# A two-layer hybrid backbone in one kernel: the MLPs' way down moved between the pairs of the way up, its gated adds moved to accumulating DMAs, and a padded layout for the convolution

## The chip, the core and the metric

One core of a Trainium2 chip runs the whole kernel. The metric is the device time of one execution in microseconds (us). Before the change it is 2623.2 us, the median of 3 runs (2618.38 to 2624.76).

Engines are named as the profile names them: PE (TensorE, matmul), PEld (its weight load), DVE (VectorE), ACT (ScalarE), POOL (GpSimd) and SP (SyncE, which issues most DMAs).

## The reference, cut to what matters

640 tokens (128 of a prompt, 512 of a latent grid) of width 1024 pass two layers. Each layer is a block of three mixers, which the change leaves alone, and a gated MLP of inner width 2816:

```python
xn2 = rmsnorm(x, norm2) * (1 + scale2) + shift2
u = dwconv3(xn2 @ w_up, ffn_conv_w)           # width 3 over positions, prompt and grid apart
a, bval = u[..., :D_FF], u[..., D_FF:]
x = x + gate2 * ((jax.nn.silu(a) * bval) @ w_down)
```

After the second layer a last rmsnorm gives the output.

## The kernel before, in words

**Layout.** Channels lie on the 128 partitions, the 640 tokens (T) along the free axis, in two halves of 320 (HALF), since one matmul fills 320 columns of a PSUM bank. Every f32 operand is split in two parts, `hi` and `lo` (ACT casts `hi`, L116; DVE subtracts for `lo`, L117), and a product takes three matmuls for each block of 128 x 128 weights: hi·hi, hi·lo, lo·hi (L149 to L151, L473 to L475). A weight tile `wraw` or `T` (128 x 512: four blocks) is loaded on SP's queue and split into `whi` and `wlo`, of which 6 are kept (`WB`).

**The way up** makes 22 pairs of a gate and a value column block (`NFF`). A pair would take 8 products of half the depth (4 blocks) by half the tokens, 96 matmuls; `pair_steps` (L477) does it in 7, 84 matmuls, by a scheme of sums of weights (L497) and sums of activations (`T3`, `t2`, `T4`, `t1`, made once for each MLP by `Forms.second`, L442). `B11`, `B21` are the first token half of the normalised input (made by `Forms.first` while the layer's output projection still runs), `B12`, `B22` the second. The pieces are collected from PSUM banks `Y`, `X`, `Z` into `o` and `z` (ACT copies L504, L523, L529, L534, L543; DVE adds L513, L531, L535). Then `ffn_conv` (L966) makes the convolution (one ACT product L968, then on DVE two taps for each of two segments, L970 and L972), and `ffn_act` (L976) silu, product and split into `fh`, `fl`.

**The way down** runs in 4 parts (`FFPARTS`: pairs 0 to 4, 5 to 10, 11 to 16, 17 to 21). When a part's pairs, and the first pair of the next part, are done, all 8 output blocks m of that part follow in one piece: `product` into a bank from `ps.any()`, then `add_gated` (L560 to L563) adds gate times product to `x[m]` on DVE, in 3 instructions for each m. The last part is done by token halves, with the squares for the next norm and the next norm's steps (`first`) between. The first 3 pairs (`LEAD`) do their `B11` and `B21` products ahead, since those need the first token half only.

**In layer 0** `ada_rows` (L308) also runs in the MLP: 12 loads of rows of `w_ada`, each with two long DVE products (L320).

**Order.** A scheduler orders each engine's instructions by when they can run in its own model and by the order in the code, and gives out the buffers. Each engine then runs its list strictly in order. The scheme's first waits are therefore set by where a `wlo` split stands in DVE's list.

Of the kernel before, what the change touches and what calls it, by code (L numbers as in the profile page):

```python
# [16 lines left out]
P = 128  # L17
# [28 lines left out]
DMA_ADDS = False  # L46
LEAD = 3
# [3 lines left out]
FFPARTS = ((0, 5), (5, 11), (11, 17), (17, 22))  # L51
# [6 lines left out]
def hybrid_flow_kernel(ctx: ExitStack, tc: tile.TileContext, a: dict):  # L58
# [109 lines left out]
    class ps:  # L168
# [4 lines left out]
        BUFS = {"mla": {"sc": 2, "pt": 2}, "hgrn": {"sc": 2, "m": 1, "ad": 1}, "ffn": {"Y": 2, "Z": 2, "X": 2}}  # L173
# [37 lines left out]
        @staticmethod  # L211
        def any():

            ps.turn += 1
            tag = ("lin", "X", "Z", "Y")[ps.turn % 4]
            return (ps.bank() if tag == "lin" else ps.one(tag))[:, 0:HALF]
# [192 lines left out]
    class Forms:  # L409


        def __init__(self, l, which, sq, xf):
            self.l, self.which, self.sq, self.xf = l, which, sq, xf
            self.f = {n: [None, None] for n in ("B11", "B21", "B22", "t1", "t2", "T3", "T4")}
            self.raw = {}

        def put(self, name, q, f):
            if name in ("t2", "T3", "T4"):
# [23 lines left out]
        def second(self, pool):  # L442
            bc = self.sq.rstd(1)
            raw = self.raw
            for q in range(2):
                for n, name in enumerate(("B12", "B22")):
                    f = raw[name, q] = form_tile(pool, F32, "fh", "xn", 7)
                    for e in range(2):
                        norm_raw(self.l, self.which, self.sq, 1, f, e, KH * n + 2 * q + e, bc)
                f = raw["T3", q] = form_tile(pool, F32, "fl", "xs", 7)  # L450
                V.tensor_tensor(f, raw["B22", q], raw["B12", q], ALU.subtract)
                self.put("T3", q, f)
            for q in range(2):
                f = raw["t2", q] = form_tile(pool, F32, "fl", "xs", 7)
# [10 lines left out]
            for q in range(2):  # L465
                self.put("B22", q, raw["B22", q])
# [10 lines left out]
    def pair_steps(l, g, F, pool, lead, banks, evict):  # L477
# [3 lines left out]
        def load(src, own=False):  # L481
            t = (pool.tile([P, 512], F32, tag="T", name="T", bufs=LEAD) if own else
# [10 lines left out]
        def add(t, src, tile=None):  # L493
            if DMA_ADDS:
                G.dma_start(t, src, accum_op=ALU.add)
            else:
                V.tensor_tensor(t, t, tile, ALU.add)  # L497

        h0, h1 = half(0), half(1)
        o0 = pool.tile([P, T], F32, tag="o", name="o", bufs=4)  # L500
        t = load(wa, True)
        Y = banks[0]()
        part_product(Y, form(t), F.operand("B11"), True, False)
        S.copy(o0[:, h0], Y)  # L504

        rb = None

        def second():
            nonlocal rb
            rb = load(wb)  # L510
            X = banks[1]()
            part_product(X, form(rb), F.operand("B21"), True, True)
            V.tensor_tensor(o0[:, h0], X, o0[:, h0], ALU.add)  # L513
        if lead:
            second()
        yield
        o1 = pool.tile([P, T], F32, tag="o", name="o", bufs=4)
        rc = load(wc)
        add(t, wc, rc)
        Z = banks[2]()  # L520
        part_product(Z, form(t), F.operand("T3"), True, False)
        z = pool.tile([P, HALF], F32, tag="z", name="z", bufs=2)
        S.copy(z, Z)  # L523
        if not lead:
            second()
        rd = load(wd)
        add(t, wd, rd)
# [4 lines left out]
        add(rc, wd, rd)  # L532
# [433 lines left out]
    def ffn_conv(g, o, fp, fconv):  # L966
        u = fp.tile([P, T], F32, tag="u", name="u", bufs=3)
        S.mul(u, o, fconv[:, 1, g:g + 1])  # L968
        for s0, s1, s in ALLSEGS:
            V.scalar_tensor_tensor(u[:, s0 + 1:s1], o[:, s0:s1 - 1], fconv[:, 0, g:g + 1], u[:, s0 + 1:s1],  # L970
                                   ALU.mult, ALU.add)
            V.scalar_tensor_tensor(u[:, s0:s1 - 1], o[:, s0 + 1:s1], fconv[:, 2, g:g + 1], u[:, s0:s1 - 1],  # L972
                                   ALU.mult, ALU.add)
        return u

    def ffn_act(ua, ub, fp):  # L976
        S.activation(ua, ua, AF.Silu)
# [84 lines left out]
    for l in range(DEPTH):  # L1062
# [126 lines left out]
        with pool_of("fp") as fp:  # L1189
# [12 lines left out]
            def up_pair(j):
                us = {}

                def evict(s, o):
                    us[s] = ffn_conv(s * NFF + j, o, fp, fconv)
                    if s == 0:
                        Ys.append(ffn_act(us[0], us[1], fp))
# [171 lines left out]
```

## Time and profile before

| | |
|---|---|
| median of 3 runs | 2623.2 us (2618.38 to 2624.76) |
| the profiled execution: its own time, its span | 2630.3 us, 2628.5 us |
| PE busy, share of the span | 2505.1 us, 95% |
| DVE busy | 1948.2 us, 74% |
| ACT busy | 1239.4 us, 47% |
| POOL busy | 117.7 us, 4% |
| granted clock of PE, mean | 0.981 |

A window's row says: its stretch in us from the span's start, its length, then busy us (and instructions) of PE, PEld, DVE, ACT and POOL, the granted clock of PE, the share of the DMA engines' time and GB/s. A timeline's row says start, duration, engine, line, operation, output and inputs, shape, count, and in brackets the idle time before it with what ended it. Matmuls overlap, and so do short instructions of DVE: the cost of one in a row of many is the distance of two starts, not its duration. A group's row ends with count, busy us, mean ns of one, and the engine's idle time before such instructions. A row of a tile gives count, duration in ns (min/median/max), first and last start.

### The profile page before, as it was taken

The numbers are of one execution on the slowest core, as the hardware profiler recorded it, in microseconds if no ns is written. First come the engines' busy times: TensorE is split into PE (matmuls) and PEld (weight loads), VectorE is DVE, ScalarE is ACT, GpSimd is POOL, SyncE is SP. The second block draws the span as 40 slices with busy tenths as digits, with TensorE's granted clock in tenths as the row PEclk, the third lists the DMA queues.
The fourth block names the chain that finished last, engine by engine and source line by source line (L and its number), as shares of the span: only waits on it lengthen the run. The fifth ranks groups of instructions, "written<-read, shape, count | busy, mean of one in ns | idle before, by whom it ended". The sixth has DMA issues, their size and how long they took to land.

```text
span 2628.5 us, 44321 instructions
## 1 busy us (share of the span) xinstructions
PE 2505.1 (95%) x16894; PEld 2424.5 (92%) x16894; DVE 1948.2 (74%) x4109; ACT 1239.4 (47%) x2492; POOL 117.7 (4%) x97
## 2 busy tenths in 40 slices
PE   7999999999999789999989999999999979999997
PEld 3999999999999679999989999999999978999997
DVE  5677787777755888887877777787774469796877
ACT  3467733333323544554654766334433346463543
POOL 1000000000111000000020000000011100000001
PEclk8999999999999899999999999999999989999999
DMA  6211243333352223222242113333332302322323
GB/s 229 72 45 45 65 133 109 108 111 106 120 151 64 88 88 98 89 73 81 72 146 59 41 41 105 110 111 117 101 108 84 119 22 85 87 80 68 90 63 102
DMA packets 142887, 242.05 MB, mean 92 GB/s; under 512 B 16913, under 2 KB 36049, under 8 KB 142545
## 3 DMA queue, kind: packets, MB, share of 16 engines
q1 hardware_dynamic: 138066, 228.73, 28.7%
q10 hardware_dynamic: 4608, 10.49, 1.3%
q8 instruction: 132, 2.16, 0.4%
q14 instruction: 81, 0.66, 0.1%
HBM read 232.56 MB, written 6.59 MB: 91 GB/s over the span
## 4 chain that ended last, share of the span: by engine, by line
PE 69%; DVE 20%; ACT 4%; DMA 4%; issue 3%; POOL 1%; DVEq 0%; ACTq 0%; SPq 0%; POOLq 0%
PE lin L149 13%; PE lin L150 13%; PE lin L151 13%; DVE wlo L117 5%; PE sc L901 2%; DVE u L970 2%; PE sc L636 2%; DVE u L972 2%; DMA wraw<-in_w_rows 2%; PE pt L927 2%; PE Y L475 2%; PE pt L918 2%; DVE ad L320 1%; ACT whi L116 1%; PE Y L473 1%
## 5 line engine op out<-in xcount | busy, mean ns | idle before, releaser
L149 PE MATMUL lin<-Xh,whi 128*128 128x320 f32 x1920 | 606.7, 316 | 6.8 <-DVE th L739 5.1
L150 PE MATMUL lin<-Xl,whi 128*128 128x320 f32 x1920 | 596.6, 311 | 0.0
L151 PE MATMUL lin<-Xh,wlo 128*128 128x320 f32 x1920 | 596.2, 311 | 0.0
L116 ACT CAST whi<-wraw 128x512 fp32r<-128x512 f32 (+1 forms) x616 | 350.3, 580 | 463.4 <-PE lin L150 320.4
L117 DVE TENSOR_TENSOR wlo<-wraw,whi 128x512 fp32r<-128x512 f32 (+1 forms) x616 | 395.1, 653 | 162.7 <-ACT whi L116 155.2
L149 PEld LDWEIGHTS lin<-Xh,whi 128*128 128x128 f32 x1920 | 362.2, 189 | 9.7 <-DVE th L739 6.8
L150 PEld LDWEIGHTS lin<-Xl,whi 128*128 128x128 f32 x1920 | 362.4, 189 | 0.0
L151 PEld LDWEIGHTS lin<-Xh,wlo 128*128 128x128 f32 x1920 | 362.0, 189 | 0.0
L320 DVE SCALAR_TENSOR_TENSOR ad<-wraw,rows 128x512 f32<-128x512 f32 x296 | 211.6, 715 | 91.5 <-DMA wraw<-in_w_rows 88.1
L473 PE MATMUL Y<-Xh,whi 128*128 128x320 f32 x504 | 158.3, 314 | 4.3 <-ACT whi L116 2.4
L475 PE MATMUL Y<-Xh,wlo 128*128 128x320 f32 x504 | 157.8, 313 | 1.8 <-DVE wlo L117 1.8
L116 ACT CAST whi<-T 128x512 fp32r<-128x512 f32 x176 | 106.7, 618 | 107.8 <-DVE T L497 46.1
L474 PE MATMUL Y<-Xl,whi 128*128 128x320 f32 x504 | 156.8, 311 | 0.0
L117 DVE TENSOR_TENSOR wlo<-T,whi 128x512 fp32r<-128x512 f32 x176 | 118.9, 685 | 24.7 <-ACT whi L116 24.1
L149 PE MATMUL lin<-yh,whi 128*128 128x320 f32 x384 | 120.5, 314 | 0.7 <-ACT th L733 0.7
L475 PE MATMUL Z<-Fh,wlo 128*128 128x320 f32 x352 | 111.3, 316 | 8.0 <-DVE wlo L117 8.0
L151 PE MATMUL lin<-yh,wlo 128*128 128x320 f32 x384 | 118.8, 309 | 0.0
L150 PE MATMUL lin<-yl,whi 128*128 128x320 f32 x384 | 118.6, 309 | 0.0
L473 PE MATMUL Z<-Fh,whi 128*128 128x320 f32 x352 | 110.6, 314 | 0.0
L474 PE MATMUL Z<-Fl,whi 128*128 128x320 f32 x352 | 109.3, 311 | 0.0
L473 PEld LDWEIGHTS Y<-Xh,whi 128*128 128x128 f32 x504 | 95.7, 190 | 7.3 <-ACT o L534 3.3
L475 PEld LDWEIGHTS Y<-Xh,wlo 128*128 128x128 f32 x504 | 95.6, 190 | 3.4 <-DVE wlo L117 2.9
(346 smaller groups left out, 6181.8 us busy)
## 6 DMA issues: line engine op xcount, KB each, us to landing
wraw<-in_w_main SPq DMA_DIRECT2D x418, 256.0 KB, 2.7
wraw<-in_w_rows SPq DMA_DIRECT2D x160, 256.0 KB, 2.8
wraw<-in_w_down SPq DMA_DIRECT2D x74, 256.0 KB, 2.8
wraw<-in_w_o SPq DMA_DIRECT2D x48, 256.0 KB, 2.7
T<-in_w_main SPq DMA_DIRECT2D x44, 256.0 KB, 2.8
ada<-in_w_ada SPq DMA_DIRECT2D x24, 256.0 KB, 6.0
x<-in_xT ACTq DMA_DIRECT2D x16, 320.0 KB, 3.5
rows<-c_keep SPq DMA_DIRECT2D x8, 512.0 KB, 4.6
```

The source lines that it names most:

```text
L116: S.copy(hi, x)
L117: V.tensor_tensor(lo, x, hi.bitcast(F32), ALU.subtract)
L149: PE.matmul(o, wh, xh[:, half(j)], start=(k == 0), stop=False)
L150: PE.matmul(o, wh, xl[:, half(j)], start=False, stop=False)
L151: PE.matmul(o, wl, xh[:, half(j)], start=False, stop=(k == n - 1))
L320: V.scalar_tensor_tensor(spare(), raw, 1.0, rows[:, s], ALU.mult, ALU.mult, accum_out=part[:, j, m - m0, s:s + 1])
L473: PE.matmul(o, wh[:, c], xh, start=start and k == 0, stop=False, skip_group_check=True)
L474: PE.matmul(o, wh[:, c], xl, start=False, stop=False, skip_group_check=True)
L475: PE.matmul(o, wl[:, c], xh, start=False, stop=stop and k == KH - 1, skip_group_check=True)
L636: PE.matmul(o[:, c * P:(c + 1) * P], kc[:, c * P:(c + 1) * P], strided(QK, c * P, ((2 * hh, nb), (T + hh, 2), (1, hh))), start=True, stop= ...
L901: PE.matmul(o[:, 512 - hk + j * hk:512 + j * hk], qq[rows, tq * P:(tq + 1) * P], kk[rows, k0 + j * hk:k0 + (j + 1) * hk], start=st, stop=sp)
L918: PE.transpose(o[:, (i - c0) * P:(i - c0 + 1) * P], p[:, i * P:(i + 1) * P], ident)
```

## The change: what it does

1. **Parts.** `FFPARTS` becomes 6 parts (pairs 0 to 2, 3 to 6, 7 to 10, 11 to 14, 15 to 18, 19 to 21). The way down of all but the last is a generator, `down_steps`, and after each pair of the next part up to `-(-KD // (k1 - ahead - 1))` of its 8 slices are run: 3, 3 and 2 behind the first three of four pairs.
2. **Gated adds.** In these slices ACT multiplies the product in PSUM by the gate into a tile `g`, and POOL issues a DMA that adds `g` to `x[m]` in SBUF (40 of them for each MLP, 320 KB each). `g` takes its buffers from the tag `u` (4 instead of 3), which the convolution also uses. The last part keeps its adds on DVE.
3. **Padded layout.** `o`, `z`, `u`, `fh`, `fl` hold prompt and grid with a column of zeros between them (642 columns), so that a tap of the convolution is one DVE instruction for both segments. ACT's copies from PSUM into this layout are two where a half holds the border (128 and 192 columns) and one else. The way down's first half is 322 columns wide.
4. **Plain pairs.** `LEAD` goes; the first two pairs are made plainly, by 96 matmuls each, `B12` is split in `Forms.second` too, `B12` and `B22` first of all there.
5. Two of DVE's combinations for a pair become one over 642 columns (L528 of the new kernel), PSUM banks are Y 2, Z 1, X 1, f 2.

```diff
-FFPARTS = ((0, 5), (5, 11), (11, 17), (17, 22))
+FFPARTS = ((0, 3), (3, 7), (7, 11), (11, 15), (15, 19), (19, 22))
@@ pair_steps
-        S.copy(o1[:, h0], Y)
-        part_product(Z, form(rd), F.operand("T4"), False, True)
-        V.scalar_tensor_tensor(o1[:, h0], Z, -1.0, o1[:, h0], ALU.mult, ALU.subtract)
+        put_half(o1, Y, 0)
+        part_product(Z, form(rd), F.operand("T4"), False, True)
+        put_half(z, Z, 0)
...
-        S.copy(o1[:, h1], Y)
-        V.scalar_tensor_tensor(o1[:, h1], o1[:, h1], -1.0, z, ALU.mult, ALU.subtract)
+        put_half(o1, Y, 1)
...
+        V.scalar_tensor_tensor(o1[:, 1:1 + TP], o1[:, 1:1 + TP], -1.0, z[:, 1:1 + TP], ALU.mult, ALU.subtract)
@@ ffn_conv
-        S.mul(u, o, fconv[:, 1, g:g + 1])
-        for s0, s1, s in ALLSEGS:
-            V.scalar_tensor_tensor(u[:, s0 + 1:s1], o[:, s0:s1 - 1], fconv[:, 0, g:g + 1], u[:, s0 + 1:s1],
...
+        S.mul(u, o[:, 1:1 + TP], fconv[:, 1, g:g + 1])
+        V.scalar_tensor_tensor(u, o[:, 0:TP], fconv[:, 0, g:g + 1], u, ALU.mult, ALU.add)
+        V.scalar_tensor_tensor(u, o[:, 2:2 + TP], fconv[:, 2, g:g + 1], u, ALU.mult, ALU.add)
@@ the MLP
+            for n, j, tag in ((0, 0, "lin"), (1, 0, "lin"), (2, 0, "Y"), (0, 1, "Y"), (1, 1, "X"), (2, 1, "Z"),
+                              (3, 0, "f"), (3, 1, "f")):
+                if j == 0:
+                    held[n] = weights(w_main(l, G_UP + n))
+                o = (ps.bank() if tag == "lin" else ps.one(tag))[:, 0:HALF]
+                for k, ((wh, wl), (xh, xl)) in enumerate(zip(held[n], B[j], strict=True)):
...
+                put_half(os_[n], o, j)
+                if j == 1:
+                    finish(n // 2, n % 2)
+
+            def down_steps(k0, k1):
+                for m in range(KD):
+                    W = weights([a["w_down"][l, m][:, k * P:min(k + 4, k1) * P] for k in range(k0, k1, 4)])
+                    g = fp.tile([P, T], F32, tag="u", name="g", bufs=4)
+                    for j in range(2):
+                        o = ps.any()
+                        down_product(o[:, 0:FHALF[j].stop - FHALF[j].start], W, Ys[k0:k1], j)
+                        for c, s0, s1, s in FSEGS[j]:
+                            S.mul(g[:, s0:s1], o[:, c:c + s1 - s0], modT[l][:, 40 + m, s:s + 1])
+                    G.dma_start(x[m], g, accum_op=ALU.add)
+                    yield
...
+                for j in range(ahead, k1):
+                    next(ups[j])
+                    if j + 1 < NFF:
+                        next(ups[j + 1])
+                    run(ups[j])
+                    run(steps, 2)
+                    run(down, -(-KD // max(1, k1 - ahead - 1)))
```

DVE's list at the start of layer 0's MLP, before: the `Forms` (`xn`, `xs`, `Fl`, `Xl`), one sum for pair 0 (L513) and the first weight split (`wlo`) behind them, for pair 1's `B21` product.

```order
L117 TENSOR_TENSOR Fl_9567<-xs_9553,Fh_9566 128x640
L117 TENSOR_TENSOR Fl_9572<-xs_9559,Fh_9571 128x640
L463 TENSOR_TENSOR xn_9537<-xn_9370,xn_9537 128x640
L513 TENSOR_TENSOR o_9597<-X_9620,o_9597 128x320
L117 TENSOR_TENSOR wlo_9663<-wraw_9659,whi_9662 128x512
L117 TENSOR_TENSOR Xl_9582<-xn_9537,Xh_9581 128x640
```

And now, at the same place: six taps of the first three blocks' convolutions (L959, L960) and a product (L966) stand between the `Forms` and the next weight splits, those of the fourth plain block (`wlo_9841`, `wlo_9847`); the first three blocks' six splits have moved ahead of the norm's chain.

```order
L464 TENSOR_TENSOR xn_9539<-xn_9370,xn_9539 128x640
L116 TENSOR_TENSOR Xl_9593<-xn_9521,Xh_9592 128x640
L959 SCALAR_TENSOR_TENSOR u_9768<-o0_9605,fconv_9603,u_9768 128x642
L116 TENSOR_TENSOR Xl_9598<-xn_9539,Xh_9597 128x640
L960 SCALAR_TENSOR_TENSOR u_9768<-o0_9605,fconv_9603,u_9768 128x642
L959 SCALAR_TENSOR_TENSOR u_9798<-o1_9606,fconv_9603,u_9798 128x642
L959 SCALAR_TENSOR_TENSOR u_9834<-o2_9607,fconv_9603,u_9834 128x642
L960 SCALAR_TENSOR_TENSOR u_9798<-o1_9606,fconv_9603,u_9798 128x642
L960 SCALAR_TENSOR_TENSOR u_9834<-o2_9607,fconv_9603,u_9834 128x642
L966 TENSOR_TENSOR u_9768<-u_9768,u_9798 128x642
L116 TENSOR_TENSOR wlo_9841<-wraw_9838,whi_9840 128x512
L116 TENSOR_TENSOR wlo_9847<-wraw_9844,whi_9846 128x512
```

ACT's list in layer 1, before: from one pair into the next, copies out of PSUM, casts, the convolution's first product (L968) and silu (L977).

```order
L504 COPY o_26103<-Y_26106 128x320
L116 CAST whi_26175<-wraw_26172 128x512
L543 COPY o_25947<-Y_25950 128x320
L968 ACTIVATE u_26137<-o_25947,fconv_24028 128x640
L523 COPY z_26170<-Z_26153 128x320
L116 CAST whi_26195<-T_26104 128x512
L116 CAST whi_26212<-wraw_26192 128x512
L116 CAST whi_26230<-wraw_26150 128x512
L977 ACTIVATE u_26137<-u_26137 128x640
```

And now, behind a pair: the gate products of three slices of the way down (L1232, `g`) stand among the casts and silu (L965), each of them waiting for its own matmuls.

```order
L481 COPY o2_24012<-Y_27126 128x320
L115 CAST whi_27477<-T_27277 128x512
L958 ACTIVATE u_27311<-o2_24012,fconv_24008 128x642
L1232 ACTIVATE g_27327<-lin_27328,mod1_78 128x128
L1232 ACTIVATE g_27327<-lin_27328,mod1_78 128x192
L115 CAST whi_27495<-wraw_27474 128x512
L1232 ACTIVATE g_27327<-f_27343,mod1_78 128x320
L965 ACTIVATE u_27311<-u_27311 128x642
L1232 ACTIVATE g_27364<-lin_27365,mod1_78 128x128
L1232 ACTIVATE g_27364<-lin_27365,mod1_78 128x192
L115 CAST fh_27317<-u_27311 128x642
```

The four parts of DVE's gated adds before the last are gone from its list, and POOL's list, which held nothing in an MLP up to its last part, now holds one DMA for each `g`.

## Rows read from the trace of the kernel before

**Rows 1.** Windows: each MLP up to its first way-down matmul, and from there.
```profile
856.20:970.90 114.70, 89.08 (x521) 83.50 (x522) 102.94 (x199) 63.37 (x115) 0.00 (x0) 0.88 0.26 81
970.90:1342.80 371.90, 361.71 (x2409) 353.91 (x2407) 308.75 (x624) 186.64 (x361) 10.35 (x13) 1.00 0.30 89
2143.30:2245.00 101.70, 83.41 (x501) 79.32 (x502) 93.28 (x169) 61.38 (x111) 0.00 (x0) 0.89 0.22 65
2245.00:2614.20 369.20, 362.45 (x2431) 355.59 (x2430) 298.97 (x589) 182.71 (x349) 7.96 (x8) 1.00 0.28 83
```

**Rows 2.** Instructions by tile `fh`: layer 0's first and last, layer 1's first.
```profile
L149 PE MATMUL X<-fh,whi x88: 306/309/472, 971.1 to 1334.2; 128*128 128x320 f32 x88
L151 PE MATMUL Y<-fh,wlo x88: 307/309/418, 975.8 to 1342.6; 128*128 128x320 f32 x88
L149 PE MATMUL X<-fh,whi x88: 304/309/418, 2245.0 to 2606.7; 128*128 128x320 f32 x88
```

**Rows 3.** Timeline, TensorE: end of layer 1's MLP, seven matmuls in a row.
```profile
2612.76 0.31 PE L151 MATMUL lin<-fh,wlo 128*128 128x320 f32 x1
...
2613.64 0.31 PE L151 MATMUL lin<-fh,wlo 128*128 128x320 f32 x1
```

**Rows 4.** Timeline, TensorE: start of layer 0's MLP.
```profile
852.63 0.28 PE L239 MATMUL lin<-ones,acc 128*128 128x2 f32 x2
...
856.21 0.63 PE L473 MATMUL Y<-Xh,whi 128*128 128x320 f32 x1 [0.41 <-ACT whi L116]
...
866.98 0.31 PE L474 MATMUL lin<-Xl,whi 128*128 128x320 f32 x1
878.23 0.64 PE L475 MATMUL X<-Xh,wlo 128*128 128x320 f32 x1 [10.94 <-DVE wlo L117]
```

**Rows 5.** Waits of TensorE in layer 0's MLP, the largest.
```profile
PE X L475 <- DVE wlo L117: 12.3, 2, 10.9
```

**Rows 6.** Timeline, VectorE: start of layer 0's MLP.
```profile
861.32 2.84 DVE L405 SCALAR_TENSOR_TENSOR xn<-x,amul,lin 128x320 f32<-128x320 f32 x6 [0.87 <-PE lin L251]
...
877.50 0.68 DVE L117 TENSOR_TENSOR wlo<-wraw,whi 128x512 fp32r<-128x512 f32 x1
878.09 2.29 DVE L117 TENSOR_TENSOR Xl<-xn,Xh 128x640 fp32r<-128x640 f32 x3
```

**Rows 7.** Timeline, VectorE: a convolution and two gated adds, layer 0.
```profile
1301.54 1.01 DVE L970 SCALAR_TENSOR_TENSOR u<-o,fconv,u 128x127 f32<-128x127 f32 x2 [0.70 <-ACT u L968]
1302.47 1.01 DVE L972 SCALAR_TENSOR_TENSOR u<-o,fconv,u 128x127 f32<-128x127 f32 x2
...
1310.62 0.66 DVE L562 SCALAR_TENSOR_TENSOR x<-Z,mod,x 128x128 f32<-128x128 f32 x2
1311.20 0.67 DVE L562 SCALAR_TENSOR_TENSOR x<-Y,mod,x 128x128 f32<-128x128 f32 x2
```

**Rows 8.** Windows of 20 us in layer 1: a way down, then pairs.
```profile
2260.00:2280.00 20.00, 20.00 (x138) 20.00 (x137) 11.10 (x26) 4.74 (x10) 0.00 (x0) 1.00 0.28 81
2320.00:2340.00 20.00, 18.64 (x117) 16.84 (x116) 19.47 (x36) 13.25 (x24) 0.00 (x0) 1.00 0.19 53
```

**Rows 9.** Groups by shape, VectorE, layer 0's MLP: the rows of w_ada.
```profile
L320 DVE SCALAR_TENSOR_TENSOR pr<-wraw,rows 128x512 f32<-128x512 f32 x24 | 16.0, 684 | 0.3 <-DMA rows<-c_keep 0.3
```

**Rows 10.** Groups by shape, ScalarE, layer 1's MLP.
```profile
L523 ACT COPY z<-Z 128x320 f32<-128x320 f32 x22 | 9.3, 422 | 6.7 <-PE Z L475 6.7
L116 ACT CAST whi<-wraw 128x128 fp32r<-128x128 f32 x21 | 6.2, 293 | 0.3 <-PE Z L150 0.2
```

**Rows 11.** DMA issues of 320 KB: KB each, median us to landing.
```profile
x<-in_xT ACTq DMA_DIRECT2D x16, 320.0 KB, 3.5
x_keep<-x ACTq DMA_DIRECT2D x8, 320.0 KB, 2.9
```

**Rows 12.** Windows: the last part of each MLP's way down.
```profile
1298.70:1342.80 44.10, 41.23 (x272) 39.01 (x270) 38.73 (x96) 25.40 (x61) 10.18 (x10) 1.00 0.45 133
2574.90:2614.20 39.30, 37.00 (x246) 35.19 (x244) 31.54 (x77) 16.81 (x39) 7.96 (x8) 1.00 0.37 110
```

More of the change, by code (lines that the diff above doesn't have):

```diff
@@ L37 @@
 WB = 6
+FHB = 7
 RAWB = 4
@@ L214, in any @@
             ps.turn += 1
-            tag = ("lin", "X", "Z", "Y")[ps.turn % 4]
-            return (ps.bank() if tag == "lin" else ps.one(tag))[:, 0:HALF]
+            return ps.bank() if ps.turn % 2 else ps.one("f")
     def rsqrt_small(out, m, n):
@@ L491, in form, with add @@
             return hi, lo
[L493 to L500, printed above, removed]
+        def add(t, other):
+            V.tensor_tensor(t, t, other, ALU.add)
         t = load(wa, True)
-        Y = banks[0]()
+        Y = ps.one("Y")[:, 0:HALF]
         part_product(Y, form(t), F.operand("B11"), True, False)
-        S.copy(o0[:, h0], Y)
@@ L506, in pair_steps @@
[L506 to L515, printed above, removed]
+        put_half(o0, Y, 0)
         yield
-        o1 = pool.tile([P, T], F32, tag="o", name="o", bufs=4)
         rc = load(wc)
-        add(t, wc, rc)
-        Z = banks[2]()
+        add(t, rc)
+        Z = ps.one("Z")[:, 0:HALF]
@@ L521, in pair_steps @@
         part_product(Z, form(t), F.operand("T3"), True, False)
[L522 to L525, printed above, removed]
+        put_half(z, Z, 1)
+        rb = load(wb)
+        X = ps.one("X")[:, 0:HALF]
+        part_product(X, form(rb), F.operand("B21"), True, True)
+        for c0, c1, off in PADS[0]:
+            V.tensor_tensor(o0[:, c0 + off:c1 + off], X[:, c0:c1], o0[:, c0 + off:c1 + off], ALU.add)
         rd = load(wd)
-        add(t, wd, rd)
+        add(t, rd)
@@ L1202, in up_pair @@
[L1202 to L1208, printed above, removed]
-                return pair_steps(l, G_UP + 2 * j, F, fp, j < LEAD,
-                                  [bank(t) for t in (("Y", "X", "Z") if j != 2 else ("lin", "lin", "Z"))], evict)
-            ups = [up_pair(j) for j in range(NFF)]
-            for j in range(LEAD):
-                next(ups[j])
+            os_ = [fp.tile([P, TP + 2], F32, name=f"o{i}") for i in range(4)]
@@ new lines, in hybrid_flow_kernel, with finish @@
+            zs = fp.tile([P, TP + 2], F32, name="z")
+            for t in os_ + [zs]:
+                for c0, c1 in ((0, 1), (TC + 1, TC + 3), (TP + 1, TP + 2)):
+                    G.memset(t[:, c0:c1], 0.0)
+            Ys, us = [], {}
+            def finish(j, s):
+                us[s] = ffn_conv(s * NFF + j, os_[2 * (j % 2) + s], fp, fconv)
+                if len(us) == 2:
+                    Ys.append(ffn_act(us[0], us[1], fp))
+                    us.clear()
+            B = [F.operand("B11", "B21"), F.operand("B12", "B22")]
@@ L1214, in hybrid_flow_kernel @@
+            ups = [pair_steps(l, G_UP + 2 * j, F, fp, os_[2 * (j % 2)], os_[2 * (j % 2) + 1], zs,
+                              lambda s, j=j: finish(j, s)) for j in range(NFF)]
+            next(ups[PLAIN])
+            down = iter(())
             for pi, (k0, k1) in enumerate(FFPARTS):
                 last = pi == len(FFPARTS) - 1
-                for j in range(k0 + (pi > 0), k1 + (not last)):
+                ahead = max(k0, PLAIN)
+                for j in range(ahead, k1):
                     next(ups[j])
-                    if LEAD <= j + 1 < NFF:
+                    if j + 1 < NFF:
@@ L1220, in hybrid_flow_kernel @@
                         next(ups[j + 1])
                     run(ups[j])
-                    run(steps, 1)
+                    run(steps, 2)
+                    run(down, -(-KD // max(1, k1 - ahead - 1)))
+                run(down)
+                if not last:
+                    down = down_steps(k0, k1)
                 if l == 0 and last:
```

118 lines of the change are left out of this document (61 added, 57 removed).

## Prediction, made before the changed kernel ran

> **What bounds the kernel now.** I read the page's shares first: PE is busy 95% of the span. That is a mean, so I took windows next, each MLP up to its first way-down matmul and from there [rows 1, 2]. Layer 0's MLP is 114.7 + 371.9 = 486.6 us long, layer 1's 101.7 + 369.2 = 470.9 us. In the second stretch PE is busy 97 to 98% at clock 1.00. In the first, the clock is 0.88 and 0.89, and DVE is busy 103 of 115 and 93 of 102 us.
>
> To see how much could be won, I count matmuls. Six steps at full clock take 0.88 us, so one costs 0.147 us [rows 3]. An MLP has 22 pairs of 84 and 1056 matmuls on the way down (8 blocks x 2 halves x 22 x 3), 2904 or 426 us. The excess is 60.6 us in layer 0 and 44.9 us in layer 1. Up to the first way-down matmul six pairs are made, 504 matmuls or 73.9 us: there the excess is 40.8 and 27.8 us. The rest (2400 matmuls, 352.1 us) has 19.8 and 17.1 us. So most of the excess sits in a quarter of the MLP.
>
> Why it sits there, two views show. The timeline of the start [rows 4]: PE ends the output projection at 852.6, starts the MLP at 856.2, and soon waits 10.94 us for the split `wlo`; two such waits are layer 0's largest [rows 5]. On DVE that split starts at 877.50 [rows 6], behind the norm's chain (six `xn`, 2.84 us) and the `Forms`. And windows of 20 us inside layer 1 [rows 8]: in pairs DVE is busy 19.47 us and PE waits; on the way down PE is full and DVE busy 11.10. The two kinds of work have different bounds and run one after the other, so the pairs ahead of the first part run at DVE's pace, with nothing else for PE.
>
> **The change, part by part.**
> *Plain pairs.* They cost 2 x 12 = 24 more matmuls, 3.5 us for each MLP; the 322-column half adds about 0.5 us (two columns of 320 on half of 1056 matmuls). The matmul sum becomes 430 us.
>
> *DVE.* A gated add took 0.58 us for a piece [rows 7]. With three pieces and their short steps I reckon 1.05 us for each m and part; 24 fewer (three parts of 8) save 25 us. A tap fell from a pair of instructions of 0.93 us [rows 7] to one over 642 columns, which I take at the 0.74 us of a 640-column split [rows 6]: two taps for 44 blocks save about 16 us. The two plain pairs spare some 11 us of sums, fewer `wlo` splits another 4. Against that stands `B12`'s split, 1.5 us. In all some 54 us less of DVE for each MLP.
>
> *ACT.* 40 slices of gate products: copies of 320 columns take 0.422 us and 128 x 128 casts 0.293 [rows 10], so a slice has 0.42 + 0.29 + 0.35 = 1.07 us, 42 us for an MLP. Split copies of the pieces add about 20. ACT then has some 300 of 450 us: busy, not the bound by this sum.
>
> *Interleaving.* A cycle of four pairs and eight slices of a four-pair part is 336 + 192 matmuls: 77.4 us for PE. A pair costs DVE 14.0 us now (19.47 x 84 / 117 [rows 8]), less 0.7 each for the taps and the merged combination; ACT 9.5 the same way, plus 1.2 for the divided copies. With 0.6 us for a slice's weight split on each, DVE's share is 4 x 12.6 + 8 x 0.6 = 55 us, ACT's 4 x 10.7 + 8 x (1.07 + 0.6) = 56 us. PE bounds the cycle with 28% to spare, where now DVE bounds the pairs. I leave 4 us of waits for the middle of each MLP.
>
> *Accumulating DMAs.* The trace shows none. From below: off the path, a slice's `g` is needed again only four users of the tag later, over 12 us. From above: plain DMAs of 320 KB land in 2.9 to 3.5 us [rows 11]; how much longer one that adds takes, no row bounds, and the last rival prices it. I take the row it is nearest to, and so nothing on the path: 9.7 us lie between two of them (77.4 / 8), and an `x[m]` is added to again only a part later. What it costs if that cover is gone is the rival below. The Trainium skill (DMA: Bandwidth & Descriptors, section "Anatomy of one DMA — SWDGE (gpsimd) path") fits 2.0 us plus bytes over 436 GB/s to such DMAs; for 320 KB that is an estimate of 2.75 us, near the row's 2.9, and it leaves the sum as it is.
>
> *The start.* First halves of blocks 0 to 2, 72 matmuls, stand straight behind the output projection: PE starts at 852.8 and is fed to 863.4, over the norm's chain, which now ends near that time since its neighbours' `wlo` splits are ahead of it. Then PE follows `B12` and `B22` (2 x 4 splits, some .74 us each [rows 6]) and loses 2.5 us. The fourth block's split is then late: DVE starts the chain at about 860.7 (0.6 us, one split, sooner than 861.32), and ahead of that split stand 8 steps of 0.46 us, 18 of 0.74, six taps at 0.74, a product at 0.7, about 1 us of waits and one split of 0.6 [rows 6]. That is 23.8 us, so 884.5, where PE would be at 878: a stall of 6 us. The sums of pair 3 stand behind pair 2's convolution: 3 us in layer 1, 4.4 in layer 0. The rows of w_ada (24 products, 684 ns [rows 9]) stay in layer 0 and cost it 6 more while the pairs have no way down beside them. After idle time the clock is low: in the first stretch PE is busy 15.2 and 9.5 us longer than its matmuls need [rows 1]. I take 2 us for the one stall left. That is 21 us of excess up to the mixed cycle in layer 0 and 14 in layer 1, in place of 40.8 and 27.8.
>
> *The last part* stays on DVE, by halves. Its windows before are 44.1 and 39.3 us [rows 12], over 240 matmuls (35.2 us): 8.9 and 4.1 us of excess. It now has three pairs, 144 matmuls, 21.1 us, while DVE's adds, squares and the next norm's steps are as many: DVE needs some 18 us for the second half's work, PE 10.6. Also fewer matmuls (24) cover the last pair's convolution, silu and split. I take 10 and 5.5 us.
>
> *Sum.* Excess 21 + 4 + 10 = 35 in layer 0 and 14 + 4 + 5.5 = 23.5 in layer 1, over 430 us of matmuls: the MLPs become 465 and 453.5 us. The gains are 21.6 and 17.4, and each MLP's matmuls start about 0.7 us earlier: 40.4 us. From the profiled execution's own 2630.3 that gives 2589.9. It ran 7.1 us above the median of 2623.2, so on the median's scale the forecast is 2583 us.
>
> **The rivals.**
> *The start shrinks to what the order allows at best.* If the fourth split comes earlier in time than I reckon and pair 3 does not wait, the start's excess is about 10 and 6 us and the middle about 1: 25 us less than the sum, about 2558. For it: the order moves three splits ahead of the chain. Against: six taps stand before the fourth.
>
> *ACT paces the cycle.* Gate products are queued on ACT in order, each behind its own matmuls; a cast or a silu behind one waits too, and DVE and PE wait for those. With 0.25 us lost for each of 80 slices the gain shrinks by 20 us: about 2603. At 0.5 us it is 40 us, 2623, no change that can be told (a measurement of this kernel can tell 0.3%, 7.9 us, from no change: 2615 to 2631). For it: ACT is busy 13.25 of 20 us in pairs already [rows 8]. Against: four banks, two `bank()` and two `f`, let PE go two products ahead.
>
> *The DMAs are too slow: slower than before.* All go through one queue. While one takes less than 9.7 us (77.4 / 8) in a row, the queue keeps up. Beyond it `g` runs out, ACT waits, behind it everything. Price: 8 x (D - 9.7) for each of 10 parts; the 40 us are used up at D = 10.2 us, and at 10.8 the time is about 2671. For it: no row shows this kind of DMA, and the queue's work is done by an engine that the MLP has left idle up to its last part [rows 1]. Against: plain DMAs of this size need a third of that [rows 11]. The Trainium skill bears on it: DMA: Bandwidth & Descriptors, section "SWDGE vs HWDGE vs iDMA", says that an accumulating DMA can only go through GpSimd's software descriptors, which it writes to rings in SBUF, and that VectorE in a two-port mode locks it out of that. SBUF — State Buffer, section "Who interferes with whom", says that `tensor_tensor`, the form of the splits here, has no such mode and contends with GpSimd's reads alone. No run shows either yet; by the first rule D would grow with DVE's load, by the second it would not.
>
> **How the numbers follow.** Forecast 0.60, with its own range 2566 to 2602: down by a start at 12 and 8 us and less waiting in the middle, up by more slow matmuls after the stall and a last part at 14 and 9. Better case 0.12 (2558). ACT as the pace 0.12 at about 2603, and 0.07 at no change. DMAs 0.09, 2640 to 2700. Faster by over 0.3%: 0.60 + 0.12 + 0.12 = 0.84; same 0.07; slower 0.09. The range 2556 to 2616 leaves out the slow DMAs, no change and a few in a hundred on the low side, some 0.19.
>
> **What would show it.** Right: layer 0's first MLP matmul follows the output projection within 1 us; PE's largest wait is for a `wlo` split ahead of the fourth plain block, some 6 us in place of 10.9; no long stretch with DVE above 95% behind pair 5; DVE busy near 340 us in layer 1's MLP, ACT near 300, PE's windows in the middle at 97% or more; the MLPs 465 and 453.5 us long; DMAs from `g` to `x` landing in 3 to 6 us. Wrong: waits of ACT's gate products for `g`'s buffers (then the DMAs are at fault), waits of PE for `fh` or of DVE for silu behind a gate product (then ACT's order), or a last part more than 6 us longer than now over its matmuls.

## The result, and the profile after

The changed kernel takes 2587.5 us (median of 4 runs, 2585.24 to 2590.7) against 2621.6 us before: ratio 0.9871, interval [0.9854, 0.9888], 34 us less. The forecast was 2583, its range 2556 to 2616.

TensorE's timeline where each MLP begins, layer 0 and layer 1:

```profile
845.90 0.28 PE L237 MATMUL lin<-ones,acc 128*128 128x2 f32 x2
846.04 0.39 PE L1217 MATMUL Y<-Xh,whi 128*128 128x320 f32 x1
...
2114.71 0.28 PE L237 MATMUL lin<-ones,acc 128*128 128x2 f32 x2
2114.85 0.39 PE L1217 MATMUL Y<-Xh,whi 128*128 128x320 f32 x1
```

The first MLP matmul now follows the output projection at once; before, 3.6 us lay between [rows 4]. Layer 0's MLP starts 6.7 us earlier than in the profile before, though nothing ahead of it is changed: that profiled execution was 7 us above its median, and the profiles of all the other kernels below end this output projection at 843 to 848 us, where it did so at 852.5. The 6.7 us are no gain. I therefore measure each MLP from the last matmul of its output projection to its last way-down matmul: before 490.1 and 474.6 us, after 474.9 and 453.2. That is 15.2 and 21.4 us less. Between the MLPs 2.5 us more are won, in part since 11 matmuls of the layer that follows now stand inside layer 0's MLP, and 1 us is lost at the end.

Windows of the changed kernel: start, middle and end of layer 0's MLP, then of layer 1's.

```profile
846.04:1000.00 153.96, 135.13 (x860) 131.76 (x859) 124.09 (x222) 90.21 (x194) 7.26 (x15) 0.94 0.36 101
1000.00:1280.00 280.00, 280.00 (x1903) 280.00 (x1902) 205.44 (x322) 182.02 (x402) 27.59 (x32) 1.00 0.51 120
1280.00:1330.00 50.00, 41.26 (x249) 39.00 (x247) 36.14 (x88) 26.74 (x63) 12.40 (x15) 0.92 0.42 132
2114.85:2270.00 155.15, 149.24 (x1010) 148.69 (x1009) 127.70 (x207) 105.55 (x228) 10.06 (x26) 0.99 0.38 98
2270.00:2540.00 270.00, 268.07 (x1820) 267.65 (x1818) 193.51 (x296) 173.64 (x382) 25.03 (x29) 1.00 0.49 114
2540.00:2583.40 43.40, 26.82 (x156) 25.40 (x156) 28.07 (x79) 10.67 (x24) 7.11 (x8) 0.78 0.22 75
```

PE is idle 18.8, 0 and 8.7 us in layer 0, 5.9, 1.9 and 16.6 us in layer 1 (of these, 11.9 us stand behind the MLP). The 1.9 us is the head of the end's wait of 3.5 us, which the window's edge at 2540 cuts in two. And the same stages before:

```profile
852.70:1010.00 157.30, 126.52 (x763) 119.97 (x762) 136.50 (x283) 75.20 (x138) 0.00 (x0) 0.90 0.30 95
1010.00:1298.70 288.70, 284.54 (x1910) 279.74 (x1909) 237.82 (x448) 150.54 (x278) 0.17 (x3) 1.00 0.26 77
...
2139.20:2270.00 130.80, 109.94 (x684) 105.67 (x683) 112.08 (x215) 71.59 (x133) 0.00 (x0) 0.91 0.27 78
2270.00:2574.90 304.90, 300.45 (x2017) 295.41 (x2016) 250.46 (x473) 156.84 (x291) 0.00 (x0) 1.00 0.26 77
```

There it was idle 30.8 and 4.2 us, and 20.9 and 4.4 us. So the gain lies at the start, where the clock too is higher, 0.94 and 0.99 for 0.90 and 0.91. The middle had only 4 us of idle time to give.

TensorE's waits after, in layer 0's MLP and then in layer 1's (us in all, times, longest):

```profile
PE Y L472 <- ACT whi L115: 9.0, 3, 4.8
PE f L1219 <- DVE wlo L116: 4.8, 1, 4.8
PE lin L978 <- ACT fh L115: 3.5, 1, 3.5
PE Y L472 <- ACT o L481: 2.5, 1, 2.5
...
PE f L1219 <- DVE wlo L116: 4.8, 1, 4.8
PE lin L978 <- ACT fh L115: 3.5, 1, 3.5
PE lin L249 <- DVE dg L243: 2.9, 2, 1.7
```

The wait of 10.9 us is gone in layer 0 [rows 5] and in layer 1, where it read before:

```profile
PE X L475 <- DVE wlo L117: 10.9, 1, 10.9
```

The fourth plain block's split stands in its place, at 4.8 us. The accumulating DMAs, by their tile `g`:

```profile
L1233 POOL DMA_DIRECT2D x<-g x80: 859/862/1010, 924.4 to 2525.0; - x80
...
DMA to landing us min/median/max: 3.6/4.7/7.0
```

### The profile page after: what moved, and what is told of

It reads as the page before. It is cut to its first block, busy times and chain, and to the rows that moved or that the text cites. A ratio compares the mean times of both kernels' runs of the same rounds, so it can differ in the third digit from the quotient of the medians.

```text
span 2583.5 us, 44707 instructions
## 1 busy us (share of the span) xinstructions
PE 2491.8 (96%) x16942; PEld 2429.8 (94%) x16942; DVE 1853.4 (72%) x3711; ACT 1333.6 (52%) x2846; POOL 186.7 (7%) x207
## 4 chain that ended last, share of the span: by engine, by line
PE 81%; DVE 11%; DMA 2%; ACT 2%; issue 2%; POOL 0%; DVEq 0%; SPq 0%; ACTq 0%; POOLq 0%
PE lin L148 13%; PE lin L150 13%; PE lin L149 13%; PE Y L472 3%; PE Y L474 3%; PE Y L473 3%; PE sc L625 2%; PE sc L890 2%; PE lin L978 2%; PE f L980 2%; PE lin L979 2%; PE lin L980 2%; PE f L979 2%; PE f L978 2%; DVE wlo L116 2%
## 5 line engine op out<-in xcount | busy, mean ns | idle before, releaser
L116 DVE TENSOR_TENSOR wlo<-T,whi 128x512 fp32r<-128x512 f32 x160 | 109.7, 688 | 71.5 <-ACT whi L115 70.6
L472 PE MATMUL Y<-Xh,whi 128*128 128x320 f32 x480 | 148.6, 310 | 2.5 <-ACT o L481 2.5
L474 PE MATMUL Y<-Xh,wlo 128*128 128x320 f32 x480 | 148.3, 309 | 0.0
L473 PE MATMUL Y<-Xl,whi 128*128 128x320 f32 x480 | 148.1, 309 | 0.0
L115 ACT CAST whi<-T 128x512 fp32r<-128x512 f32 x160 | 99.0, 621 | 82.5 <-DVE T L500 21.4
L1233 POOL DMA_DIRECT2D x<-g x80 | 69.2, 864 | 772.9 <-ACT g L1232 765.3
L978 PE MATMUL lin<-fh,whi 128*128 128x322 f32 (+1 forms) x352 | 111.0, 315 | 9.3 <-ACT fh L115 7.0
L980 PE MATMUL lin<-fh,wlo 128*128 128x322 f32 (+1 forms) x352 | 110.9, 315 | 0.0
L979 PE MATMUL lin<-fl,whi 128*128 128x322 f32 (+1 forms) x352 | 110.8, 315 | 0.0
L980 PE MATMUL f<-fh,wlo 128*128 128x320 f32 (+1 forms) x352 | 110.3, 313 | 0.0
```

What stands on the lines that cost most here:

```text
L115: S.copy(hi, x)
L116: V.tensor_tensor(lo, x, hi.bitcast(F32), ALU.subtract)
L472: PE.matmul(o, wh[:, c], xh, start=start and k == 0, stop=False, skip_group_check=True)
L473: PE.matmul(o, wh[:, c], xl, start=False, stop=False, skip_group_check=True)
L474: PE.matmul(o, wl[:, c], xh, start=False, stop=stop and k == KH - 1, skip_group_check=True)
L978: PE.matmul(o, wh, fh[:, FHALF[j]], start=(k == 0), stop=False)
```

## The experiments

"MLP 0" and "MLP 1" are lengths from the last matmul of the output projection to the last way-down matmul, in the profiled execution of each. Runs were made on several chips, so kernels are compared by their ratios to the kernel before on the same chip; 0.001 is 2.6 us. The 11 matmuls of the next layer (1.6 us) lie inside MLP 0 in all but before, e6, e9, b2 and b3.

| kernel | us | ratio to before, interval | MLP 0 | MLP 1 |
|---|---|---|---|---|
| before | | 1 | 490.1 | 474.6 |
| the change | 2587.5 | 0.9871 [0.9854, 0.9888] | 474.9 | 453.2 |
| e1 one piece | 2595.2 | 0.9892 [0.9877, 0.9907] | 484.2 | 453.7 |
| e2 no relief | 2598.4 | 0.9914 [0.9896, 0.9931] | 485.8 | 456.3 |
| e3 neither | 2602.8 | 0.9923 [0.9909, 0.9938] | 488.3 | 455.8 |
| e4 one plain pair | 2605.3 | 0.9934 [0.9920, 0.9947] | 487.8 | 459.8 |
| e5 rows of w_ada later | 2581.7 | 0.9848 [0.9835, 0.9862] | 468.5 | 453.5 |
| e6 last part of four | 2574.4 | 0.9819 [0.9806, 0.9833] | 470.0 | 448.8 |
| e7 convolutions later | 2585.6 | 0.9856 [0.9839, 0.9872] | 472.9 | 452.4 |
| e8 slices spread at the end | 2572.5 | 0.9813 [0.9799, 0.9826] | 466.6 | 446.4 |
| e9 neither, four parts | 2609.0 | 0.9959 [0.9947, 0.9972] | 494.0 | 456.4 |
| b1 (e5 + e7 + e8) | 2557.7 | 0.9769 [0.9756, 0.9782] | 459.3 | 446.2 |
| b2 (e5 + e6 + e8) | 2556.4 | 0.9761 [0.9748, 0.9773] | 459.4 | 443.9 |
| b3 (b2, adds on VectorE) | 2556.3 | 0.9765 [0.9749, 0.9781] | 456.0 | 444.7 |

**e1, the way down in one piece.**

```diff
-                    run(down, -(-KD // max(1, k1 - ahead - 1)))
+                    run(down)
```

Expected: 

> The eight slices of a part's way down run in one piece behind the first pair of the next part, all else as in the changed kernel (2587.5 us). Theory (the working of the prediction): pairs and way down have different bounds, and a pair alone now needs 12.6 us on VectorE against 12.3 on TensorE, so without the mixture the pairs fall slightly behind again: 0.4 us or so for each of 20 pairs and some waits at each change, 8 us for each MLP, about 2604. Rival A (the mixture carries nearly all of the gain): the pairs run at VectorE's pace as before, 2615 to 2620. Rival B (VectorE's relief alone carries it, the mixture nothing): 2584 to 2592.

Measured 0.0021 above the change, 5.5 us, with intervals that overlap. The profile puts it in layer 0 (484.2 for 474.9; the stretch to the next MLP gives 2 us back); layer 1 does not notice. Against the changed kernel's 2587.5 that is 2593: 11 us under the theory's 2604, just above rival B's 2584 to 2592. The theory priced it too high and at both layers; rival A falls.

**e2, VectorE's relief undone.**

```diff
-                            S.mul(g[:, s0:s1], o[:, c:c + s1 - s0], modT[l][:, 40 + m, s:s + 1])
-                    G.dma_start(x[m], g, accum_op=ALU.add)
+                            V.scalar_tensor_tensor(x[m][:, s0:s1], o[:, c:c + s1 - s0],
+                                                   modT[l][:, 40 + m, s:s + 1], x[m][:, s0:s1], ALU.mult, ALU.add)
...
+            for s0, s1 in ((0, TC + 1), (TC + 1, TP)):
+                V.scalar_tensor_tensor(u[:, s0:s1], o[:, s0 + i:s1 + i], fconv[:, i, g:g + 1], u[:, s0:s1],
```

Expected: 

> The slices stay between the pairs, but VectorE's relief is undone: the gated adds of the slices are made on VectorE straight from PSUM (no gate products on ScalarE, no accumulating DMAs), and each tap is two instructions (129 and 513 columns). Theory: a cycle of four pairs and eight slices costs VectorE 55 + 8.4 + 3 = 66 of 77.4 us, still under TensorE, so nearly nothing is lost in the middle; the start and the last pairs lose 2 us or so, 2587 to 2594. Rival A agrees. Rival B (the relief carries the gain): VectorE gets some 33 us more work for each MLP, 66 in all, and the time comes back to 2615 or more.

Measured 0.0043 above, 11 us: more than the theory's, far from rival B's. Again layer 0 pays (485.8), layer 1 little (456.3). The adds and the taps were undone together here; b3 undoes the adds alone, and what the taps in one instruction are worth alone no run shows.

**e3, both undone.** The two edits together.

Expected: 

> Both undone: way down in one piece, gated adds on VectorE, taps in two instructions; what stays of the change is the plain start, six parts and one merged combination. Theory: pairs are again at VectorE's pace, the middle loses what it lost before and more since the way down's adds cannot run beside pairs: 2605 to 2615, the start's gain (10 us or so for each MLP) being all that is left. Rival A: the same as with one piece alone, within 4 us. Rival B: the same as with no relief alone.

Measured 0.0052 above, 14 us, 2 us under the theory's 2605 to 2615. It stands 0.0031 (8 us) above e1, which speaks against rival A's 4 us; from e2 it is not clearly apart, as rival B has it. Its profile settled more than its time. Windows of e3 in layer 1:

```profile
2240.00:2300.00 60.00, 60.00 (x407) 59.92 (x407) 51.47 (x101) 30.00 (x62) 0.00 (x0) 1.00 0.30 88
2300.00:2400.00 100.00, 100.00 (x682) 99.92 (x681) 88.12 (x166) 57.38 (x124) 0.00 (x0) 1.00 0.27 77
2400.00:2550.00 150.00, 150.00 (x1018) 149.84 (x1018) 129.64 (x247) 79.01 (x168) 0.00 (x0) 1.00 0.28 81
```

Without the mixture and without the relief, PE is full through layer 1's middle. VectorE's work in this MLP is 394 us, as much as before (392 [rows 1]). So in layer 1 neither is what filled it.

**e4, one plain pair.**

```diff
-PLAIN = 2
+PLAIN = 1
...
-            for n, j, tag in ((0, 0, "lin"), (1, 0, "lin"), (2, 0, "Y"), (0, 1, "Y"), (1, 1, "X"), (2, 1, "Z"),
-                              (3, 0, "f"), (3, 1, "f")):
+            for n, j, tag in ((0, 0, "lin"), (1, 0, "lin"), (0, 1, "Y"), (1, 1, "X")):
```

Expected: 

> Only the first pair is made plainly, the second by seven products (12 matmuls fewer for each MLP, 1.8 us). Theory: the first token halves that cover the norm's chain shrink from 72 to 48 matmuls (10.6 to 7.1 us), and the second pair's sums stand behind the Forms on VectorE; the start loses some 6 us for each MLP, less the 1.8: about 2596. Rival (the plain start is worth nothing, its matmuls only cost): 2584.

Measured 0.0063 above, 16.5 us, twice what the theory said, and the dearest single undoing. Both MLPs lose (12.9 and 6.6 us). More went than the text of the edit says. In the changed kernel one block's first half (24 matmuls, in bank `Y`) runs ahead of the norm's last matmuls (L249), the other two (in `lin`) behind them. In e4 both first halves are in `lin`, and none runs ahead: in layer 0 PE waits 1.6 and 3.5 us there (1.2 in the changed kernel), and the first MLP matmul comes 8.1 us behind the output projection in place of 0.3. One plain pair with another bank was not run. PE's largest wait in layer 1 is now in pair 1, for a split behind the `Forms`:

```profile
PE Z L474 <- DVE wlo L116: 6.4, 1, 6.4
```

**e5, the rows of w_ada later.**

```diff
-                    run(steps, 2)
+                    run(steps, 2 if j >= 7 else 0)
```

Expected: 

> The changed kernel (ratio 0.9871 to before), but the rows of w_ada in layer 0's MLP start behind pair 7 instead of pair 2, where the way down already runs beside the pairs. Theory: beside pairs 3 to 6 they are on the path, since those pairs have too little way down beside them and ScalarE and VectorE are late; waits of 11 us and the low clock behind them stand there in layer 0 alone. Moved, they are hidden: 8 to 14 us faster, ratio 0.982 to 0.984. Rival (the waits there come from the start, which hands its lateness on, and layer 0's are only longer by chance): under 3 us, ratio 0.986 to 0.987.

Measured 0.0023 below the change, 6 us, between theory and rival; the intervals overlap, but the profile puts the difference where it belongs: layer 0 is 6.4 us shorter, layer 1 the same. The waits for `whi` fall from 9.0 to 4.6 us and not to nothing. Windows show why. In the changed kernel the rows' products run from 899.7 to 1008 us, in e5 from 984.8 to 1103. The changed kernel in layer 0, e5 before and beside the rows, and the changed kernel in layer 1, which has no such rows:

```profile
882.00:1010.00 128.00, 115.09 (x739) 112.27 (x738) 101.34 (x183) 74.90 (x169) 7.91 (x9) 0.96 0.43 118
...
882.00:984.00 102.00, 102.00 (x697) 102.00 (x696) 84.52 (x131) 72.70 (x162) 7.03 (x8) 1.00 0.44 112
984.00:1104.00 120.00, 111.68 (x727) 109.82 (x726) 90.31 (x164) 67.16 (x151) 9.94 (x12) 0.97 0.48 128
...
2152.00:2530.00 378.00, 378.00 (x2570) 378.00 (x2569) 282.57 (x435) 250.34 (x555) 34.53 (x40) 1.00 0.49 116
```

Where the rows stand PE is idle, 12.9 us in the changed kernel and 8.3 us in e5; where they do not, it is full. So the waits move with the rows, and the theory's word that they are hidden beside the way down fails: e5 gets a third of their cost back, not all (layer 0 has 20.8 us more than layer 1 over its matmuls up to the last part in the changed kernel, 13.9 in e5). How a row's products reach PE, three queues show. The changed kernel, VectorE, ScalarE and TensorE ahead of its first such wait:

```profile
901.73 0.68 DVE L318 SCALAR_TENSOR_TENSOR pr<-wraw,rows 128x512 f32<-128x512 f32 x1
902.34 0.88 DVE L960 SCALAR_TENSOR_TENSOR u<-o,fconv,u 128x642 f32<-128x642 f32 x1
903.14 0.68 DVE L318 SCALAR_TENSOR_TENSOR pr<-wraw,rows 128x512 f32<-128x512 f32 x1
904.02 0.83 DVE L966 TENSOR_TENSOR u<-u 128x642 f32<-128x642 f32 x1
905.04 0.68 DVE L500 TENSOR_TENSOR T<-T,wraw 128x512 f32<-128x512 f32 x1
...
903.25 0.74 ACT L965 ACTIVATE u<-u 128x642 f32<-128x642 f32 x1 [1.84 <-DVE u L960]
904.88 0.73 ACT L115 CAST fh<-u 128x642 fp32r<-128x642 f32 x1 [0.89 <-DVE u L966]
905.75 0.62 ACT L115 CAST whi<-T 128x512 fp32r<-128x512 f32 x1
...
906.42 0.64 PE L472 MATMUL Y<-Fh,whi 128*128 128x320 f32 x1 [3.72 <-ACT whi L115]
```

The cast that PE needs starts when VectorE's sum `T` ends (905.72), and that sum stands behind the taps and the rows' products (0.6 us each, four of them between 899.7 and 903.8). ScalarE's silu and split wait for the same taps.

**e6, a longer last part.**

```diff
-FFPARTS = ((0, 3), (3, 7), (7, 11), (11, 15), (15, 19), (19, 22))
+FFPARTS = ((0, 3), (3, 7), (7, 11), (11, 15), (15, 18), (18, 22))
```

Expected: 

> The last two parts are pairs 15 to 17 and 18 to 21 instead of 15 to 18 and 19 to 21. Theory (the last part is too short for VectorE's adds and the next norm): 48 more matmuls, 7 us, in the last part, and the wait at the end shrinks by 3 us or so for each MLP: 4 to 8 us faster in all, ratio 0.984 to 0.986. Rival (the last part's length does not matter, since the norm's chain behind it is a chain of short steps): within 3 us, ratio 0.986 to 0.988.

Measured 0.0052 below, 13.6 us, more than the theory's 4 to 8. The wait for the last pair's split shrinks only from 3.5 to 2.2 us in each MLP.

**e7, the first convolutions later.**

```diff
-                if j == 1:
-                    finish(n // 2, n % 2)
+            for n in range(4):
+                finish(n // 2, n % 2)
```

Expected: 

> The convolutions of the first two pairs are written behind the fourth plain block's products, so that VectorE makes that block's weight split ahead of the taps. Theory: PE's wait of 4.8 us ahead of the fourth block goes in both MLPs, with the slow matmuls behind it; part of it comes back as a later convolution: 4 to 10 us faster in all, ratio 0.983 to 0.986. Rival (VectorE's whole queue is the limit there, order inside it changes nothing): within 3 us; the wait reappears ahead of pair 2 or 3.

Measured 0.0015 below, with intervals that overlap: unclear, and 2.0 and 0.8 us in the two MLPs by the profiles. PE's wait ahead of the fourth block is gone, and layer 1's first way-down matmul comes 6 us sooner, but new waits of 1.6 and 0.9 us stand behind and the end is the same. The rival is nearer. That VectorE's and ScalarE's whole queues are late there, and not one split, fits this but was not tested apart.

**e8, slices spread over the last stretch.**

```diff
-                    run(down, -(-KD // max(1, k1 - ahead - 1)))
+                    run(down, -(-KD // max(1, k1 - ahead - (not last))))
```

Expected: 

> In the last part's stretch the slices of the part before are run 3, 3 and 2 behind its three pairs, instead of 4 and 4 behind the first two. Theory: the wait of 3.5 us for the last pair's split ahead of the last part, and the low clock behind it (0.73 to 0.84 in those windows), go: 6 to 12 us in both MLPs together, ratio 0.983 to 0.985. Rival (what is won there is lost again because VectorE then stands further behind in the last part): within 3 us, ratio 0.986 to 0.988.

Measured 0.0058 below, 15 us, more than the theory's 6 to 12; 8.3 and 6.8 us in the two MLPs. The wait itself was 3.5 us in each. Windows show the rest. The changed kernel, at and behind that wait in layer 1, then e8 at about the same work:

```profile
2536.00:2544.00 8.00, 4.52 (x23) 4.26 (x23) 5.16 (x9) 3.11 (x6) 0.00 (x0) 0.79 0.09 26
2544.00:2548.00 4.00, 4.00 (x19) 4.00 (x18) 2.40 (x9) 2.72 (x7) 1.53 (x2) 0.57 0.00 0
```

```profile
2532.00:2536.00 4.00, 4.00 (x29) 4.00 (x28) 3.14 (x9) 1.93 (x4) 2.60 (x4) 1.00 0.19 58
2536.00:2540.00 4.00, 4.00 (x32) 4.00 (x30) 2.81 (x7) 2.06 (x5) 0.50 (x1) 1.00 0.00 0
```

Behind the wait the granted clock is 0.57, near the lower of its two levels (1.2 of 2.4 GHz), and 4 us hold 19 matmuls in place of 29. In all 21 matmuls there stand 0.27 us apart in place of 0.147: 2.7 us lost besides the wait's 3.5. The two small waits behind it (0.7 us each, for VectorE's adds) stay.

**e9, e3 with the four old parts.** The first and the last part grow with the others.

```diff
-FFPARTS = ((0, 3), (3, 7), (7, 11), (11, 15), (15, 19), (19, 22))
+FFPARTS = ((0, 5), (5, 11), (11, 17), (17, 22))
```

Expected: 

> As with neither mixture nor relief (ratio 0.9923 to before), and with the four parts of before (5, 6, 6 and 5 pairs) in place of six. Theory (new, from the profiles of the runs so far): layer 1's middle is as full without mixture and relief as with them, so what closed it is the length of a part: over four pairs VectorE falls behind by four times its excess over TensorE and catches up in the next way down; over six it falls behind so far that PE waits. Then layer 1's MLP is 5 to 10 us longer again, layer 0's as much, and only the start's gain stays; but the last part has five pairs, which gives 6 us or so back: ratio 0.993 to 0.998. Rival (the merged combination and the divided copies closed the middle, the parts' length plays no role): the middle stays full, and the longer last part gains: ratio 0.987 to 0.991.

Measured 0.9959, inside the theory's range and 9 us above e3. Its windows in layer 1 where e3's were full:

```profile
2300.00:2400.00 100.00, 98.39 (x659) 96.98 (x658) 77.25 (x149) 50.23 (x107) 0.00 (x0) 1.00 0.27 82
2400.00:2540.00 140.00, 138.38 (x932) 136.98 (x932) 117.27 (x222) 76.63 (x167) 0.00 (x0) 1.00 0.26 76
```

PE misses 3 us here again, and layer 0 is 5.7 us longer (its waits for `whi` are 22.2 us in 7 places). Layer 1's MLP as a whole is only 0.6 us longer, as its longer last part gives back what the middle loses.

**b1, b2 and b3, the edits together.** b1 is e5, e7 and e8, b2 is e5, e6 and e8, b3 is b2 with the adds of e2 (its taps stay one instruction).

Expected of b1: 

> Three edits together: the rows of w_ada behind pair 7 (alone 0.9848), the first convolutions behind the fourth plain block (alone 0.9856), the slices of the last stretch spread 3, 3, 2 (alone 0.9813), against 0.9871 of the changed kernel. They stand at three places; if the places are independent, the ratios add: 0.977 to 0.979. Rival (the start hands lateness on, and the convolutions put later only move a wait): the first edits give half of that or less, 0.980 to 0.982.

Expected of b2: 

> The rows of w_ada behind pair 7, the slices of the last stretch spread, and the last parts of three and four pairs (alone 0.9819). Theory: spreading and the longer last part share one wait (the last pair's split), but the longer part also relieves VectorE's adds and norm steps: 0.975 to 0.978. Rival (both only remove the same wait): 0.979 to 0.981.

Expected of b3: 

> The same as the run before in this list, but the gated adds of the slices on VectorE from PSUM: no gate products on ScalarE, no accumulating DMAs. Theory: VectorE has room in the mixed cycle (some 63 of 77 us), so the accumulating DMAs are worth little once the start and the end are mended: within 4 us of the run with them, ratio at most 0.0015 above. Rival (they are needed; undoing them with the taps cost 11 us in the changed kernel): 8 us or more slower, 0.003 above or more.

Measured 0.9769, 0.9761 and 0.9765. The edits of b1 add up (0.0023 + 0.0015 + 0.0058 below 0.9871 is 0.9775). In b2 the sum would be 0.9738, as it would be if e6 and e8 share part of a wait. b3 equals b2 within the noise: the 80 accumulating DMAs and 240 gate products are worth nothing that can be told. b1 to b3 cannot be told apart and are the fastest here; b2 is 0.0239 or 63 us below before and 0.0110 or 29 us below the change. What is left in its MLPs, layer 0 (beside the rows of w_ada) and then layer 1:

```profile
PE Y L472 <- ACT whi L115: 4.6, 1, 4.6
PE Y L472 <- ACT o L481: 4.5, 3, 2.0
...
PE f L1219 <- DVE wlo L116: 4.8, 1, 4.8
PE lin L249 <- DVE dg L243: 4.2, 2, 3.0
PE lin L237 <- DVE acc L350: 1.8, 1, 1.8
```

## Why the prediction was right

The time was 4.5 us above the forecast, and the likeliest case came. The gain of 34 us is 6 under the 40 forecast. Layer 1's MLP was forecast at 453.5 us and is 453.0 from its first matmul; layer 0's at 465 and is 474.7. The excess of a stage (its length less 0.147 us for each matmul of 320 columns) shows which terms were right. Start is up to the first way-down matmul (918.1 and 2179.0 us), the last part begins with its first way-down matmul (1284.5 and 2532.4):

| excess, us | forecast, layer 0 and 1 | measured, layer 0 and 1 |
|---|---|---|
| start | 21 and 14 | 17.4 and 9.5 |
| middle | 4 and 4 | 13.5 and 0.6 |
| last part | 10 and 5.5 | 12.0 and 12.8 |

- **The total is in part luck.** In layer 1 a start and a middle priced 8 us too high cancel a last part priced 7 us too low. In layer 0 the middle is missed by 9.5 us, and a slip in the sum, some 6 us, hides most of it: the forecast lengths count from a first matmul at 852.8, 3.4 us earlier than before [rows 4], and in layer 1 4 us earlier, but the sum adds 0.7 us for each. With 3.4 and 4 it would have been about 2577.
- **The start** is right as the place of the gain. The first MLP matmuls run straight behind the output projection, though 24 of them and not 72 stand ahead of the norm's last matmuls (L249), and the one stall left is the fourth block's split: at 875.51 on VectorE, forecast 884.5 in a profile that ran 6.7 us later, so 2.3 us too late; 4.8 us of wait for 6. In layer 1 pair 3 did not wait at all, where 3 us were priced.
- **The rows of w_ada** are the step that failed in layer 0. The prediction priced them only while the pairs have no way down beside them, 6 us (7 with pair 3's later sums); there layer 0 has 7.9 us more excess than layer 1, which is right. Beside the way down it priced them at nothing, and there layer 0 has 12.9 us more. e5 shows that these waits follow the rows wherever they stand. No run leaves the rows out of the MLP.
- **The middle** of layer 1 is full, where 4 us of waits were left for it. The reason given, pairs at VectorE's pace against a way down at PE's, does not carry it: it came from one window of pairs [rows 8], and over the whole middle PE was already 98 to 99% busy before. e1 to e3 show that mixture and relief matter in layer 0 (9 to 13 us), where VectorE also has the rows, and little in layer 1 (at most 3 us). And e3 against e9 shows that shorter parts fill layer 1's middle without either.
- **The accumulating DMAs** were priced at nothing on the path: right. One lands in 4.7 us, at most 7.0, under the 9.7 from which the slow rival starts. That rival fell. Nor does the time grow with VectorE's load, which the prediction left open: the 40 DMAs with VectorE the less busy beside them (40% on average) landed in 4.71 us, the other 40 (75%) in 4.76, medians both. The Trainium skill's fit (DMA: Bandwidth & Descriptors, "Anatomy of one DMA — SWDGE (gpsimd) path") gave an estimate of 2.75 us; the measured 4.7 decides. b3 adds that their gain is nothing too.
- **VectorE and ScalarE**: 341.6 and 289 us of work in layer 1's MLP (to 2568), forecast about 340 and 300. ScalarE did not become the pace.
- **The last part** was forecast 10 and 5.5 us late, with VectorE as its bound. In layer 1 it is later than that, and one sign of being wrong came with it: 6.2 us more excess than before (12.8 for 6.6 by the same count). The cause is mostly another: all eight slices are run behind the first two of its three pairs, so nothing covers the last pair's convolution, silu and split. e8 shows it with one edit: the last part's excess falls to 4.5 and 5.1 us.

## What to carry to other kernels

A wait at the start or the end of a stage can cost TensorE more than itself, since slow matmuls follow it (here 1.5 to 2.9 us behind waits of 3.5 to 4.8). Look there before the steady state, and keep something for PE behind the last producer of a stage. But taking one wait away is no gain by itself: e7 removed one of 4.8 us and nothing that can be told was won. A share of busy time near 97% on a second engine in one window is no proof that it bounds the stage: sum PE's idle time over the stage first. Compare two stages that differ in one thing: layer 1 has no rows of w_ada, and that difference was the forecast's largest miss. Side work that is hidden on average can still stand in a queue ahead of what PE needs next. Where several edits are made at once, undo each alone: here the most elaborate one (gate products and accumulating DMAs) was worth nothing that can be told once the plain ones were in place.

## What the runs showed of the hardware

An accumulating DMA of 320 KB in SBUF lands in 3.6 to 7.0 us (median 4.7, 80 of them), where plain DMAs of the same size take 2.9 to 3.5 [rows 11], and holds GpSimd 0.86 us to issue. Landing did not grow with VectorE's busy share (medians 4.71 and 4.76 us at 40% and 75%). In the changed kernel's MLPs six waits of PE of 3.5 to 4.8 us were followed by 11 to 21 matmuls some 0.27 us apart, against 0.147 at full clock (1.5 to 2.9 us lost); behind a wait of 2.5 us (up to 958.5) the granted clock was 1.00. Behind the wait of 3.5 us in layer 1 the granted clock was 0.57 for 4 us; e8, which took that wait away in both layers, made the MLPs 8.3 and 6.8 us shorter.
